# First phase of a decoder-layer kernel: a hand-written order, norm statistics by token, and low parts of the up weights on GpSimd

## The chip, the cores and the metric

The kernel runs on one core of a Trainium2 chip. The time is that of one execution on the device, in microseconds. The core has five engines that run side by side and wait for each other through semaphores: TensorE (PE, with its weight loads as PEld), VectorE (DVE), ScalarE (ACT), GpSimd (POOL) and SyncE (SP), which here only issues DMAs.

## What is computed

One decoder layer for 256 tokens of width 1024, in float32: a first feed-forward block, a mixer, a second feed-forward block, each with a norm modulated by a conditioning vector c. The change touches the beginning of the first feed-forward block alone:

```python
mod = silu(c) @ ada_w + ada_b                    # nine rows of 1024: sh1, sc1, g1, ...
n = x * rsqrt(mean(x * x, axis=-1) + EPS) * norm_ffn1_w
u = n * (1 + sc1) + sh1
gate, up = split(u @ ffn1_w_in, 2)               # ffn1_w_in: 1024 x 5632
h = x + 0.5 * g1 * ((silu(gate) * up) @ ffn1_w_out)
```

## The kernel before

**Layout and precision.** Activations lie with features on partitions: x is the tile h, 128 partitions x 8 slices x 256 tokens. A float32 product is made of three matmuls in a faster type. Each operand is split into a high part, rounded to that type, and a low part, the remainder (`half`: `act.copy(hi, v)` on ScalarE at line 128, the subtraction on VectorE at line 129). `mm3` then adds high x high (L137), low activation x high weight (L138) and high activation x low weight (L139). Weights, wst, come as high wh and low wl; activations u as uh and ul.

**The first phase** (tile pool `ep`) projects u onto the first seven tiles of 128 columns of the gate half and of the up half at once. It runs over the eight slices of 128 input features (`kt`). A slice needs two rows of ada_w of 512 KB each (`ada01`, for sc1 and sh1), and 2 x 896 weight columns, 896 KB (`w01`, gate columns at j = 0, up columns at j = 1). On VectorE, `ada_dots` (L181) multiplies such a row with silu(c), held on all partitions as cb, and sums it; `am` (L395) and `modc` (L398) are scale and shift of the slice, t (L401) is x times scale times the norm factor rb. ScalarE makes uh (L222), VectorE ul (L223). Then come 42 matmuls (seven tiles, gate and up, three each), into seven accumulators that stay open over all eight slices. wh and wl have four buffers each, two slices' worth; ada and wst four.

**Statistics and cb.** silu(c) is spread over partitions by products of ones with crow, the vector c on one partition (L362), and a silu from PSUM. For the norm, ScalarE squares x, VectorE adds the squares of all slices but for partitions (L378 to L382), a product with ones (L384) sums over partitions, ScalarE takes the root into rb (128 x 256), VectorE the reciprocal (L417). Between them stand products of ones with ones whose result nobody reads (`warm`, L368).

**What sets the order.** A scheduler with its own cost estimates sets every engine's order of instructions; the program text gives it only dependencies and priorities. SP's queue takes its loads in the order of the text. Behind the phase, silu(gate) * up is formed (L300), and the next weights are split by `half` for `pair_project`.

Of the kernel before, what the change touches and what calls it, by code (L numbers as in the profile page):

```python
# [32 lines left out]
V_N1, V_N2, V_N3, V_AB = 0, 8, 16, 24  # L33
# [10 lines left out]
HALF_BUFS = 4  # L44
SLOTS = 17
WIDE_BUFS = 3
F1 = 7
# [32 lines left out]
def layer(ctx: ExitStack, tc: tile.TileContext, a, out, packing):  # L80
    nc = tc.nc
    pe, act, dve = nc.tensor, nc.scalar, nc.vector

    cst = ctx.enter_context(tc.tile_pool(name="cst", bufs=1))
    wp = ctx.enter_context(tc.tile_pool(name="wp", bufs=1))
# [36 lines left out]
    def half(v):  # L122
        nk, n = v.shape[1], v.shape[2]
        hi = wp.tile([P, 1024], F32R, tag="wh", name=nm("wh"), bufs=HALF_BUFS)
        lo = wp.tile([P, 1024], F32R, tag="wl", name=nm("wl"), bufs=HALF_BUFS)
        hi = hi[:, :nk * n].rearrange("p (k n) -> p k n", k=nk)
        lo = lo[:, :nk * n].rearrange("p (k n) -> p k n", k=nk)
        act.copy(hi, v)  # L128
        last_lo[0] = dve.tensor_tensor(lo, v, hi.bitcast(F32), ALU.subtract).ins  # L129
        return hi, lo  # L130
# [5 lines left out]
    def mm3(o, l, r, first, last, skip=False):  # L136
        pe.matmul(o, l[0], r[0], start=first, stop=False, skip_group_check=skip)  # L137
        pe.matmul(o, l[0], r[1], start=False, stop=False, skip_group_check=skip)  # L138
        pe.matmul(o, l[1], r[0], start=False, stop=last, skip_group_check=skip)  # L139

    def at(pair, *idx):
        return pair[0][idx], pair[1][idx]
# [17 lines left out]
    def table(name):  # L160
        ins = act.preload_act_table_set(name).ins  # L161
# [12 lines left out]
    modc = cst.tile([P, N_MOD, KD], F32, name="modc")  # L174
# [4 lines left out]
    def ada_dots(st, j, f0):  # L179
        for i in range(st.shape[1]):  # L180
            dve.scalar_tensor_tensor(st[:, i, :], st[:, i, :], 1.0, cb, ALU.mult, ALU.mult,  # L181
                                     accum_out=raw[:, j, f0 + i:f0 + i + 1])
# [37 lines left out]
    def u_tile(u, f, t, jsh):  # L220
        sh = modc[:, jsh, f:f + 1]
        act.activation(u[0][:, f, :], t, AF.Identity, bias=sh)  # L222
        dve.scalar_tensor_tensor(u[1][:, f, :], t, sh, u[0][:, f, :].bitcast(F32),  # L223
                                 ALU.add, ALU.subtract)
# [109 lines left out]
                each()  # L334

    w1 = "ffn1_w_in"
    with tc.tile_pool(name="ep", bufs=1) as ep:
        table("silu_and_others")
        crow = ep.tile([1, D], F32, name="crow")
        nc.sync.dma_start(crow, a["c"])  # L340
# [17 lines left out]
        sts = [ada01(0)]  # L358
        wst = [w01(0)]
        for q in range(2):  # L360
            ps = misc_ps()
            pe.matmul(ps, ones[0:1, :], crow[:, q * 512:(q + 1) * 512], start=True, stop=True)  # L362
# [7 lines left out]
        warm(12)  # L370
        bias1 = ep.tile([P, KD], F32, name="bias1")
        dve.tensor_scalar(bias1, col[:, V_AB + KD:V_AB + 2 * KD], 1.0, None, ALU.add)
        table("sqrt_and_others")
        sqs = []
        for i in range(2):
            sq = ep.tile([P, 4, T], F32, tag="sq4", name=nm("sq4"), bufs=2)
            act.activation(sq, h[:, 4 * i:4 * i + 4, :], AF.Square)
            dve.tensor_tensor(sq[:, 0:2, :], sq[:, 0:2, :], sq[:, 2:4, :], ALU.add)  # L378
            sqs.append(sq)
        dve.tensor_tensor(sqs[0][:, 0:2, :], sqs[0][:, 0:2, :], sqs[1][:, 0:2, :], ALU.add)  # L380
        ssq = sqs[0][:, 0, :]
        dve.tensor_tensor(ssq, ssq, sqs[0][:, 1, :], ALU.add)  # L382
        ps = misc_ps()
        pe.matmul(ps[:, :T], ones, ssq, start=True, stop=True)  # L384
        rb = ep.tile([P, T], F32, name="rb")
        lookup(rb, ps[:, :T], AF.Sqrt, bias=epsc, scale=1.0 / D)
        warm(12)
        table("silu_and_others")
        u = new_u()
        am = sp.tile([P, KD], F32, tag="am", name=nm("am"), bufs=2)  # L390

        def u_first(kt, st, between=lambda: None):
            ada_dots(st[0], 1, kt)
            between()
            dve.scalar_tensor_tensor(am[:, kt:kt + 1], raw[:, 1, kt:kt + 1], bias1[:, kt:kt + 1],  # L395
                                     col[:, V_N1 + kt:V_N1 + kt + 1], ALU.add, ALU.mult)
            ada_dots(st[1], 0, kt)
            dve.tensor_tensor(modc[:, 0, kt:kt + 1], raw[:, 0, kt:kt + 1],  # L398
                              col[:, V_AB + kt:V_AB + kt + 1], ALU.add)
            t = ep.tile([P, T], F32, tag="t1", name=nm("t1"), bufs=2)  # L400
            dve.scalar_tensor_tensor(t, h[:, kt, :], am[:, kt:kt + 1], rb, ALU.mult, ALU.mult)  # L401
            u_tile(u, kt, t, 0)

        def halves(st):
            return [half(st[:, j:j + 1, :]) for j in range(2)]
# [5 lines left out]
        def first_mms(kt, j, hv):  # L411
            for f in range(F1):
                bank, slot_ = (banks[f // 2][j], f % 2) if f < 6 else (last, j)
                mm3(bank[:, slot_, :], at(hv, al, 0, slice(f * P, (f + 1) * P)), at(u, al, kt),
                    kt == 0 and slot_ == 0, kt == KD - 1 and slot_ == 1, skip=True)

        u_first(0, sts.pop(), lambda: dve.reciprocal(rb, rb))  # L417
        hw = halves(wst.pop())
        for kt in range(KD):
            if kt + 1 < KD:  # L420
                st = ada01(kt + 1)
                wt = w01(kt + 1)
                u_first(kt + 1, st)
                hw_next = halves(wt)
            first_mms(kt, 0, hw[0])
            first_mms(kt, 1, hw[1])
            hw = hw_next
    with tc.tile_pool(name=nm("fp"), bufs=1, reuse_waits="tile") as fp:
        ah = fp.tile([P, NF, T], F32R, name=nm("ah"))
# [6 lines left out]
        for p2 in range(4, NF // 2 + 1):  # L436
# [5 lines left out]
            else:  # L442
                ps = split_project(w1, f0 * P, FFN + f0 * P, u)
# [34 lines left out]
    with tc.tile_pool(name="mx", bufs=1, reuse_waits="tile") as mx:  # L478
# [385 lines left out]
    with tc.tile_pool(name=nm("fp"), bufs=1, reuse_waits="tile") as fp:  # L864
# [6 lines left out]
        for p2 in range(NF // 2):  # L871
# [14 lines left out]
            if p2 == 5:  # L886
# [104 lines left out]
```

## Time and profile before

| | us |
|---|---|
| median of 3 runs (lowest to highest) | 876.75 (876.51 to 878.15) |
| profiled execution, whole time | 876.71 |
| its span in the trace | 874.9 |
| first matmul of the phase (L137) starts | 18.10 |
| last matmul of the phase (L139) starts | 59.55 |
| mean granted TensorE clock over the span | 0.996 |

The span runs from the first to the last instruction of the program in the trace; the whole time lies 1.8 us above it. Rows of the timeline read: start, duration, engine, line, operation, output <- inputs, shapes, count, and in brackets the idle time of the engine before it and what ended it.

### The profile page before, as it was taken

The numbers are of one execution on the slowest core, as the hardware profiler recorded it, in microseconds if no ns is written. First come the engines' busy times: TensorE is split into PE (matmuls) and PEld (weight loads), VectorE is DVE, ScalarE is ACT, GpSimd is POOL, SyncE is SP. The second block draws the span as 40 slices with busy tenths as digits, with TensorE's granted clock in tenths as the row PEclk, the third lists the DMA queues.
The fourth block names the chain that finished last, engine by engine and source line by source line (L and its number), as shares of the span: only waits on it lengthen the run. The fifth ranks groups of instructions, "written<-read, shape, count | busy, mean of one in ns | idle before, by whom it ended". The sixth has DMA issues, their size and how long they took to land.

```text
span 874.9 us, 16783 instructions
## 1 busy us (share of the span) xinstructions
PE 861.0 (98%) x7038; PEld 843.6 (96%) x7038; DVE 663.8 (76%) x1000; ACT 505.5 (58%) x735; POOL 0.2 (0%) x4
## 2 busy tenths in 40 slices
PE   7999999999999999999999999999999999999996
PEld 6999999999999999999999999999999999999896
DVE  6989788897989858676898677866889985555454
ACT  5455454465666588858554558655557744444343
POOL 0000000000000000000000000000000000000000
PEclk9999999999999999999999999999999999999999
DMA  9958878994655334262757664464464685545531
GB/s 369 421 211 326 299 281 313 351 337 161 233 175 188 142 145 150 95 233 87 256 182 269 229 236 157 180 230 145 163 227 168 261 331 183 187 151 187 185 105 49
DMA packets 29023, 188.00 MB, mean 215 GB/s; under 512 B 3218, under 2 KB 3602, under 8 KB 9235
## 3 DMA queue, kind: packets, MB, share of 16 engines
q1 hardware_dynamic: 28658, 186.48, 58.3%
q8 instruction: 55, 0.90, 0.4%
q10 hardware_dynamic: 288, 0.44, 0.2%
q14 instruction: 22, 0.17, 0.1%
HBM read 185.86 MB, written 1.05 MB: 214 GB/s over the span
## 4 chain that ended last, share of the span: by engine, by line
PE 93%; DVE 4%; ACT 1%; DMA 1%; issue 1%; SPq 0%; DVEq 0%; ACTq 0%
PE proj L139 28%; PE proj L138 28%; PE proj L137 28%; PE misc L205 1%; DVE wl L129 1%; PE misc L137 1%; PE misc L139 1%; PE misc L138 1%; DMA ada<-in_ada_w_dram 1%; PE misc L676 1%; PE misc L652 0%; PE misc L805 0%; PE misc L640 0%; PE misc L806 0%; PE misc L807 0%
## 5 line engine op out<-in xcount | busy, mean ns | idle before, releaser
L128 ACT CAST wh<-wst 128x1024 fp32r<-128x1024 f32 (+3 forms) x282 | 288.9, 1032 | 280.7 <-PE proj L138 191.8
L129 DVE TENSOR_TENSOR wl<-wst,wh 128x1024 fp32r<-128x1024 f32 (+3 forms) x282 | 336.3, 1200 | 124.7 <-ACT wh L128 124.1
L137 PE MATMUL proj<-uh,wh 128*128 128x256 f32 (+1 forms) x1336 | 376.8, 283 | 2.3 <-ACT uh L222 2.3
L139 PE MATMUL proj<-uh,wl 128*128 128x256 f32 (+1 forms) x1336 | 377.4, 283 | 0.8 <-DVE wl L129 0.8
L138 PE MATMUL proj<-ul,wh 128*128 128x256 f32 (+1 forms) x1336 | 375.8, 282 | 0.0
L137 PEld LDWEIGHTS proj<-uh,wh 128*128 128x128 f32 x1336 | 250.9, 188 | 3.0 <-ACT uh L222 2.5
L139 PEld LDWEIGHTS proj<-uh,wl 128*128 128x128 f32 x1336 | 252.4, 189 | 1.2 <-DVE wl L129 1.0
L138 PEld LDWEIGHTS proj<-ul,wh 128*128 128x128 f32 x1336 | 252.3, 189 | 0.5 <-issue 0.2
L137 PE MATMUL proj<-s,wh 128*128 128x256 f32 x320 | 90.6, 284 | 0.2 <-ACT s L133 0.2
L139 PE MATMUL proj<-s,wl 128*128 128x256 f32 x320 | 89.6, 280 | 0.0
L138 PE MATMUL proj<-s,wh 128*128 128x256 f32 x320 | 89.3, 279 | 0.0
L181 DVE SCALAR_TENSOR_TENSOR wst<-wst,cb 128x1024 f32<-128x1024 f32 x56 | 67.4, 1220 | 7.2 <-DMA wst<-in_ada_w_dram 6.9
L137 PEld LDWEIGHTS proj<-s,wh 128*128 128x128 f32 x320 | 60.1, 188 | 1.0 <-issue 0.5
L138 PEld LDWEIGHTS proj<-s,wh 128*128 128x128 f32 x320 | 60.2, 188 | 0.3 <-issue 0.2
L139 PEld LDWEIGHTS proj<-s,wl 128*128 128x128 f32 x320 | 60.2, 188 | 0.2 <-issue 0.2
L139 PE MATMUL proj<-ah,wl 128*128 128x256 f32 x176 | 49.1, 279 | 0.0
L137 PE MATMUL proj<-ah,wh 128*128 128x256 f32 x176 | 49.1, 279 | 0.0
L138 PE MATMUL proj<-al,wh 128*128 128x256 f32 x176 | 49.1, 279 | 0.0
L138 PE MATMUL proj<-wl,ah 128*128 128x256 f32 (+1 forms) x132 | 42.1, 319 | 0.0
L139 PE MATMUL proj<-wh,al 128*128 128x256 f32 (+1 forms) x132 | 42.1, 319 | 0.0
L137 PE MATMUL proj<-wh,ah 128*128 128x256 f32 (+1 forms) x132 | 42.1, 319 | 0.0
L161 ACT ACT_TABLE_LOAD x28 | 35.9, 1283 | 1.2 <-PEq L965 0.7
(224 smaller groups left out, 1134.4 us busy)
## 6 DMA issues: line engine op xcount, KB each, us to landing
wst<-in_mix_w_in_dram SPq DMA_DIRECT2D x52, 1024.0 KB, 4.9
wst<-in_ffn_w_in_dram SPq DMA_DIRECT2D x37, 1024.0 KB, 5.2
wst<-in_ada_w_dram SPq DMA_DIRECT2D x28, 1024.0 KB, 5.9
wst<-in_ffn_w_out_dram SPq DMA_DIRECT2D x17, 1024.0 KB, 4.9
ada<-in_ada_w_dram SPq DMA_DIRECT2D x16, 512.0 KB, 11.7
wst<-in_w_br_ssd_dram SPq DMA_DIRECT2D x8, 1024.0 KB, 4.9
wst<-in_w_br_ret_dram SPq DMA_DIRECT2D x8, 1024.0 KB, 5.0
wst<-in_ffn_w_in_dram SPq DMA_DIRECT2D x7, 896.0 KB, 12.3
```

The source lines that it names most:

```text
L128: act.copy(hi, v)
L129: last_lo[0] = dve.tensor_tensor(lo, v, hi.bitcast(F32), ALU.subtract).ins
L137: pe.matmul(o, l[0], r[0], start=first, stop=False, skip_group_check=skip)
L138: pe.matmul(o, l[0], r[1], start=False, stop=False, skip_group_check=skip)
L139: pe.matmul(o, l[1], r[0], start=False, stop=last, skip_group_check=skip)
L161: ins = act.preload_act_table_set(name).ins
L181: dve.scalar_tensor_tensor(st[:, i, :], st[:, i, :], 1.0, cb, ALU.mult, ALU.mult, accum_out=raw[:, j, f0 + i:f0 + i + 1])
L205: pe.matmul(ps[:, :T], mean_m[n], s, start=i == 0, stop=i == len(parts) - 1)
L676: pe.matmul(py[hh * 64:hh * 64 + 64, f * T + c * P:f * T + (c + 1) * P], xd[:, c, hl * 64:hl * 64 + 64], m[c][:, hl, :], start=True, stop= ...
```

## The change

Inside the first phase the order of TensorE, ScalarE, VectorE and SyncE is that of the text (`tc.manual_schedule`); GpSimd is not among them. Behind the phase the scheduler works as before.

- x is loaded first; c comes as 128 copies straight into cb, whose silu is taken in place. The identity (ident) is loaded early on ScalarE's queue.
- The loads of three slices are issued ahead of the loop, then of slice kt + 3 in step kt.
- Statistics: each block of squares, 128 features x 128 tokens, is the stationary side of a product with a column of 1/1024, so that the mean squares stand with tokens on partitions, two columns in all. Root and reciprocal work on those; dg = ident * r, and a product of ones with dg spreads the factor over partitions again. Slice 0 reads it from PSUM, the others from rb, a copy.
- In a slice, the low part of the up weights (j = 1) is subtracted by GpSimd instead of VectorE (`lows`).

```diff
-    with tc.tile_pool(name="ep", bufs=1) as ep:
+    with (tc.tile_pool(name="ep", bufs=1) as ep,
+          tc.manual_schedule(engines={e.engine for e in (pe, act, dve, nc.sync)})):
...
-        nc.sync.dma_start(crow, a["c"])
         act.dma_start(col, a["vecs"])
+        act.dma_start(ident, a["consts"][:, :P])
...
+        nc.sync.dma_start(cb, a["c"].broadcast_to([P, D]))
...
-            pe.matmul(ps, ones[0:1, :], crow[:, q * 512:(q + 1) * 512], start=True, stop=True)
-            lookup(cb[:, q * 512:(q + 1) * 512], ps, AF.Silu)
...
+        for kt in range(3):
+            sts.append(ada01(kt))
+            wst.append(w01(kt))
...
+        warm(8)
...
             act.activation(sq, h[:, 4 * i:4 * i + 4, :], AF.Square)
-            dve.tensor_tensor(sq[:, 0:2, :], sq[:, 0:2, :], sq[:, 2:4, :], ALU.add)
...
-        pe.matmul(ps[:, :T], ones, ssq, start=True, stop=True)
...
+            for f in range(4):
+                for tt in range(2):
+                    pe.matmul(ps[:, tt:tt + 1], sq[:, f, tt * P:(tt + 1) * P], mean1,
...
+        lookup(cb, cb, AF.Silu)
+        warm(5)
...
+        def lows(kt, hw, j):
+            (nc.gpsimd if j else dve).tensor_tensor(hw[1][j], wst[kt][:, j, :], hw[0][j].bitcast(F32), ALU.subtract)
...
+        scale_first(0)
+        r = ep.tile([P, 2], F32, name="r2")
+        table("sqrt_and_others")
+        lookup(r, ps[:, :2], AF.Sqrt, bias=epsc)
+        dve.reciprocal(r, r)
+        dg = ep.tile([P, 2, P], F32, name="dg")
+        dve.tensor_tensor(dg, ident.unsqueeze(1).broadcast_to([P, 2, P]),
+                          r.unsqueeze(2).broadcast_to([P, 2, P]), ALU.mult)
+        ps = misc_ps()
+        for tt in range(2):
+            pe.matmul(ps[:, tt * P:(tt + 1) * P], ones, dg[:, tt, :], start=True, stop=True)
+        warm(10)
+        shift_first(0)
+        hw = halves(0)
...
+        t = t_first(0, ps[:, :T])
+        act.copy(rb, ps[:, :T])
+        table("silu_and_others")
+        lows(0, hw, 0)
+        u_low(0, t)
+        lows(0, hw, 1)
...
         for kt in range(KD):
+            if kt + 3 < KD:
+                sts.append(ada01(kt + 3))
+                wst.append(w01(kt + 3))
             if kt + 1 < KD:
...
+                hw_next = halves(kt + 1)
+                scale_first(kt + 1)
+                shift_first(kt + 1)
+                t = t_first(kt + 1, rb)
+                lows(kt + 1, hw_next, 0)
+                u_low(kt + 1, t)
+                lows(kt + 1, hw_next, 1)
+            first_mms(kt, 0, hw)
+            first_mms(kt, 1, hw)
```

`scale_first` is the first dot and am, `shift_first` the second dot and modc, `halves` the two casts to wh, `t_first` t and uh, `u_low` ul.

TensorE at the start of the program, before; numbers behind names tell buffers apart:

```order
L362 MATMUL misc_97<-crow,ones 128x512
L362 MATMUL misc_100<-crow,ones 128x512
L368 MATMUL misc_103<-ones 128x128 x12
L384 MATMUL misc_127<-sq_6_119,ones 128x256
L368 MATMUL misc_131<-ones 128x128 x12
L137 MATMUL proj_148<-uh_145,wh_164 128x256
L137 MATMUL proj_150<-uh_145,wh_164 128x256
```

and TensorE at the same place now, with the first rows of slice 0:

```order
L362 MATMUL misc_111<-ones 128x128 x8
L377 MATMUL misc_120<-mean_109,sq_9_121 128x1 x8
L377 MATMUL misc_120<-mean_109,sq_10_131 128x1 x8
L362 MATMUL misc_142<-ones 128x128 x5
L428 MATMUL misc_161<-dg,ones 128x128 x2
L362 MATMUL misc_164<-ones 128x128 x10
L137 MATMUL proj_192<-uh_150,wh_177 128x256
L138 MATMUL proj_192<-ul_151,wh_177 128x256
L139 MATMUL proj_192<-uh_150,wl_178 128x256
```

The products with crow are gone, the one product for the statistics became sixteen of one column, and slice 0 no longer begins with seven products that need neither ul nor wl: L138 is second.

VectorE from the first dot to the first t, before:

```order
L181 SCALAR_TENSOR_TENSOR ada_91,raw<-ada_91,cb 128x1024
L378 TENSOR_TENSOR sq_7_122<-sq_7_122 128x512
L395 SCALAR_TENSOR_TENSOR am_147<-raw,bias_116,col 128x1
L380 TENSOR_TENSOR sq_6_119<-sq_6_119,sq_7_122 128x512
L181 SCALAR_TENSOR_TENSOR ada_91,raw<-ada_91,cb 128x1024
L382 TENSOR_TENSOR sq_6_119<-sq_6_119 128x256
L398 TENSOR_TENSOR modc<-raw,col 128x1
L129 TENSOR_TENSOR wl_165<-wst_94,wh_164 128x896
L129 TENSOR_TENSOR wl_169<-wst_94,wh_168 128x896
L417 RECIPROCAL rb<-rb 128x256
L181 SCALAR_TENSOR_TENSOR ada_172,raw<-ada_172,cb 128x1024
L401 SCALAR_TENSOR_TENSOR t_20_160<-h,am_147,rb 128x256
```

and VectorE at the same place now, up to ul of slice 0:

```order
L181 SCALAR_TENSOR_TENSOR ada_93,raw<-ada_93,cb 128x1024
L389 SCALAR_TENSOR_TENSOR am_152<-raw,bias_148,col 128x1
L422 RECIPROCAL r_155<-r_155 128x2
L424 TENSOR_TENSOR dg<-k,r_155 128x256
L181 SCALAR_TENSOR_TENSOR ada_93,raw<-ada_93,cb 128x1024
L394 TENSOR_TENSOR modc<-raw,col 128x1
L436 SCALAR_TENSOR_TENSOR t_21_184<-h,am_152,misc_161 128x256
L409 TENSOR_TENSOR wl_178<-wst_96,wh_177 128x896
L441 SCALAR_TENSOR_TENSOR ul_151<-t_21_184,modc,uh_150 128x256
```

The sums of squares, one low part and the next slice's dot no longer stand ahead of t, and the reciprocal has 2 columns instead of 256.

VectorE's last slice and what follows it, now:

```order
L409 TENSOR_TENSOR wl_573<-wst_454,wh_572 128x896
L441 SCALAR_TENSOR_TENSOR ul_151<-t_73_582,modc,uh_150 128x256
L129 TENSOR_TENSOR wl_705<-wst_701,wh_704 128x1024
L300 TENSOR_TENSOR s_680<-s_680,proj_193 128x512
L300 TENSOR_TENSOR s_685<-s_685,proj_195 128x512
```

Before, there were two low parts to a slice, and the two L300 stood ahead of the first low part of the next weights (L129, 128x1024); now that low part is first.

More of the change, by code (lines that the diff above doesn't have):

```diff
@@ L368, in warm @@
                 pe.matmul(ps[:, :P], ones, ones, start=True, stop=True)
[L370 to L374, printed above, removed]
+        sts, wst = [], []
+        for kt in range(3):
+            sts.append(ada01(kt))
+            wst.append(w01(kt))
+        mean1 = ep.tile([P, 1], F32, name="mean1")
+        dve.memset(mean1, 1.0 / D)
+        warm(8)
+        ps = misc_ps()
         for i in range(2):
@@ L386, in layer @@
[L386 to L388 removed]
+            for f in range(4):
+                for tt in range(2):
+                    pe.matmul(ps[:, tt:tt + 1], sq[:, f, tt * P:(tt + 1) * P], mean1,
+                              start=i == f == tt == 0, stop=i == 1 and f == 3 and tt == 1,
+                              skip_group_check=True)
+        lookup(cb, cb, AF.Silu)
+        warm(5)
+        bias1 = ep.tile([P, KD], F32, name="bias1")
@@ L398, in u_first, with halves @@
             dve.tensor_tensor(modc[:, 0, kt:kt + 1], raw[:, 0, kt:kt + 1],
                               col[:, V_AB + kt:V_AB + kt + 1], ALU.add)
+        def halves(kt):
+            st = wst[kt]
+            his, los = [], []
+            for j in range(2):
+                his.append(wp.tile([P, 1024], F32R, tag="wh", name=nm("wh"), bufs=HALF_BUFS))
+                los.append(wp.tile([P, 1024], F32R, tag="wl", name=nm("wl"), bufs=HALF_BUFS))
+            his, los = ([t[:, :F1 * P] for t in x] for x in (his, los))
+            for j in range(2):
+                act.copy(his[j], st[:, j, :])
+            return his, los
@@ new lines, in lows, with first_mms @@
+        def lows(kt, hw, j):
+            (nc.gpsimd if j else dve).tensor_tensor(hw[1][j], wst[kt][:, j, :], hw[0][j].bitcast(F32), ALU.subtract)
+        def first_mms(kt, j, hw):
+            hv = hw[0][j], hw[1][j]
+            for f in range(F1):
+                bank, slot_ = (banks[f // 2][j], f % 2) if f < 6 else (last, j)
+                mm3(bank[:, slot_, :], at(hv, al, slice(f * P, (f + 1) * P)), at(u, al, kt),
+                    kt == 0 and slot_ == 0, kt == KD - 1 and slot_ == 1, skip=True)
@@ L400, in u_first, with t_first @@
+        warm(10)
+        shift_first(0)
+        hw = halves(0)
+        rb = ep.tile([P, T], F32, name="rb")
+        def t_first(kt, rb):
             t = ep.tile([P, T], F32, tag="t1", name=nm("t1"), bufs=2)
             dve.scalar_tensor_tensor(t, h[:, kt, :], am[:, kt:kt + 1], rb, ALU.mult, ALU.mult)
-            u_tile(u, kt, t, 0)
-        def halves(st):
-            return [half(st[:, j:j + 1, :]) for j in range(2)]
+            act.activation(u[0][:, kt, :], t, AF.Identity, bias=modc[:, 0, kt:kt + 1])
+            return t
```

37 lines of the change are left out of this document (9 added, 28 removed).

## The prediction

> **What bounds the kernel now.** I read the page first, then the waits of TensorE, then the chain that ended last, then stretches of the timeline.
>
> ```profile
> PE 861.0 (98%) x7038; PEld 843.6 (96%) x7038; DVE 663.8 (76%) x1000; ACT 505.5 (58%) x735; POOL 0.2 (0%) x4
> PE 93%; DVE 4%; ACT 1%; DMA 1%; issue 1%; SPq 0%; DVEq 0%; ACTq 0%
> PE misc L362 <- DMA crow<-in_c_dram: 2.4, 1, 2.4
> PE proj L137 <- ACT uh L222: 2.3, 1, 2.3
> PE misc L384 <- DVE modc L398: 0.9, 1, 0.9
> PE proj L139 <- DVE wl L129: 0.8, 1, 0.8
> ```
>
> TensorE is busy for 98% of the span and 93% of the chain is its matmuls. Its waits of 0.8 us and more number four, and all four lie at the start or at the end of the first phase. A shorter time can therefore come only from an earlier first useful matmul, from fewer slow matmuls behind it, or from the wait of 0.8. The chain shows what holds the first matmul back.
>
> ```profile
> 2.00 6.12 DMA ada<-in_ada_w_dram
> 8.23 1.23 DVE ada L181 x2
> 10.80 1.15 DVE ada L181 x2
> 12.35 1.33 DVE wl L129 x2
> 14.27 1.75 DVE rb L417
> 16.02 1.09 DVE ada L181 x2
> ```
>
> After the first conditioning rows have landed, VectorE carries everything: two dots, the sums of squares between them, two low parts, a reciprocal of 1.75, and a dot that belongs to the *next* slice. The reader sees a queue in a poor order, not a lack of data.
>
> ```profile
> 6.04:11.43 5.39, 5.39 (x25) 5.19 (x24) 3.86 (x7) 3.87 (x4) 0.00 (x0) 1.00 1.02 410
> 12.93:15.78 2.85, 2.85 (x25) 2.65 (x23) 2.85 (x3) 1.76 (x2) 0.00 (x0) 1.00 0.99 413
> 18.10:21.70 3.60, 3.60 (x17) 3.60 (x18) 3.60 (x8) 2.08 (x3) 0.00 (x0) 0.53 0.99 412
> 21.70:50.00 28.30, 28.30 (x240) 28.30 (x239) 28.24 (x52) 12.18 (x16) 0.00 (x0) 1.00 0.98 404
> ```
>
> The columns are the stretch, its length, busy time and count of PE, PEld, DVE, ACT and POOL, the granted clock, the DMA share and GB/s. The first two stretches hold the same filler: 24 or so passes take 5.39 us, then 2.85, so a pass costs 0.21 or 0.11 us. The first 3.6 us of useful work run at a granted clock of 0.53: 17 matmuls, 0.21 us each, against 28.30/240 = 0.118 later. These 17 would have taken 2.0 us, so the slow stretch costs **1.6 us**.
>
> ```profile
> 21.95 1.22 DVE L181 SCALAR_TENSOR_TENSOR ada<-ada,cb 128x1024 f32<-128x1024 f32 x1
> 26.39 1.09 DVE L129 TENSOR_TENSOR wl<-wst,wh 128x896 fp32r<-128x896 f32 x1
> 27.40 1.22 DVE L181 SCALAR_TENSOR_TENSOR ada<-ada,cb 128x1024 f32<-128x1024 f32 x1
> 49.18 1.22 DVE L181 SCALAR_TENSOR_TENSOR ada<-ada,cb 128x1024 f32<-128x1024 f32 x1
> 18.10 0.67 PE L137 MATMUL proj<-uh,wh 128*128 128x256 f32 x2 [2.32 <-ACT uh L222]
> 59.55 0.28 PE L139 MATMUL misc<-uh,wl 128*128 128x256 f32 x1
> 60.86 0.39 PE L139 MATMUL proj<-uh,wl 128*128 128x256 f32 x1 [0.79 <-DVE wl L129]
> ```
>
> From slice 2 (21.95) to slice 7 (49.18) VectorE needs 27.23/5 = 5.45 us a slice, with no gap (28.24 of 28.30 us busy). TensorE needs 42 x 0.118 = 4.95. VectorE is thus the slower one, and only its lead keeps TensorE fed. An earlier start of TensorE alone would soon run into it. The second low part takes 27.40 - 26.39 = 1.01 of the 5.45; without it VectorE needs **4.44**, below TensorE.
>
> **The change, part by part.** The inputs come first.
>
> ```profile
> 0.73 0.35 SPq L340 DMA_DIRECT2D crow<-in_c_dram  x1
> 1.14 0.82 SPq L112 DMA_DIRECT2D h<-in_x_dram  x2
> 4.93 1.05 ACT L377 ACTIVATE sq<-h 128x1024 f32<-128x1024 f32 x1
> 10.50 0.94 ACT L128 CAST wh<-wst 128x896 fp32r<-128x896 f32 x1 [1.39 <-DMA wst<-in_ffn_w_in_dram]
> 11.62 0.94 ACT L128 CAST wh<-wst 128x896 fp32r<-128x896 f32 x1 [0.18 <-DMA wst<-in_ffn_w_in_dram]
> 17.54 0.51 ACT L222 ACTIVATE uh<-t,modc 128x256 fp32r<-128x256 f32 x1 [2.63 <-DVE t L401]
> 18.69 0.48 DVE L223 SCALAR_TENSOR_TENSOR ul<-t,modc,uh 128x256 fp32r<-128x256 f32 x1
> DMA packets 2947, 12.61 MB, mean 420 GB/s; under 512 B 324, under 2 KB 324, under 8 KB 2945
> wf<-in_norm_final_w_dram SPq DMA_DIRECT2D x1, 512.0 KB, 6.2
> h<-in_x_dram SPq DMA_DIRECT2D x2, 512.0 KB, 4.5
> 13.63 1.28 ACT L161 ACT_TABLE_LOAD   x1
> ```
>
> Without crow ahead, x goes out 0.41 us earlier. The vector c now arrives as 128 copies, 512 KB; at 420 GB/s that is 1.25 us, and it stands ahead of all weights. The one load of that form, wf, landed 6.2 us after its issue, the halves of x, as large, after 4.5; I take the 1.25 and keep 1.7 more as its upper end. Everything behind it is later by 1.25 - 0.41 = 0.84: the weight casts start at 11.34 and 12.46, the second ends at 13.4. ScalarE's order puts uh of slice 0 behind it, so uh runs from 13.4, the first matmul follows 0.56 later as at 17.54 and 18.10, and ul, behind uh, is done at 14.4. The extra load of ident, 64 KB on ScalarE's queue, is 0.15 us by the same rate. TensorE, held to the written order, takes L138 second and needs ul then: it cannot flow before **14.4**.
>
> The rest must be ready by then. The dot starts when its rows land, 8.23 + 0.84 = 9.1, and ends 1.2 later; the reciprocal of 1.75 shrinks to two columns, the sums of squares leave VectorE, and the second dot ends at about 12.2. VectorE is no longer last. ScalarE gets c's copies 1.25 before the rows, at 7.9; their silu (like a square, 1.05) and the table of 1.28 bring it to the root at 10.2. TensorE's own queue is the tight one: 8 fillers, 16 products of one column, 5 fillers, 2 products with dg, 10 fillers. A filler is two passes.
>
> ```profile
> 2.36 3.75 PE L362 MATMUL misc<-crow,ones 1*128 1x512 f32 x4 [2.36 <-DMA crow<-in_c_dram]
> 292.20 0.53 PE L607 MATMUL misc<-av,k 128*128 128x32 f32 x4
> 292.56 0.39 PE L610 MATMUL misc<-av,ones 128*128 128x32 f32 x2
> ```
>
> The nearest row for the one-column products has 32 columns: four passes start within 0.36 us at full speed, 0.09 to 0.11 each, as much as a filler of 128, so the load of the stationary tile sets it. At the slow pace it is between that (if the load keeps its speed) and double. Thirty-two passes are 3.2 us fast and up to 6.4 slow. The fillers start at 2.35, where TensorE starts now, and end 16 x 0.21 later, near 5.9; x is squared by then (4.93 - 0.41 + 1.05 = 5.6). If the pace rises as before, after 5.4 us of work, at 7.8, nine passes are slow and 23 fast: the statistics end at 10.2, five fillers at 11.3, the products with dg at 11.8, ten fillers at **14.1**. Root, reciprocal and dg, of 2, 2 and 256 columns (ul's 256 took 0.48), fit beside the five fillers. So the first matmul runs at about 14.1, the flow starts at 14.6 with a little slack added, and it starts fast. TensorE's gain is 18.1 - 14.6 = 3.5 and the slow stretch, 1.6.
>
> The matmuls of slice 0 lose nothing else: before, seven L137 were put ahead to hide ul's lateness, now the fillers hide it. If they were too few, TensorE would idle at most from 14.1 to 14.4.
>
> GpSimd then has one low part a slice, which no row of this trace shows.
>
> ```profile
> L129 DVE TENSOR_TENSOR wl<-wst,wh 128x896 fp32r<-128x896 f32 x16 | 17.3, 1088 | 0.1
> L417 DVE RECIPROCAL rb<-rb 128x256 f32<-128x256 f32 x1 | 1.7, 1747 | 0.0
> ```
>
> The nearest row is the same subtraction on VectorE, 1.09 us; the farthest is the slowest rate per column on the page, the reciprocal's 1.747/256, which gives 6.1 for 896. I take something near the first, up to twice it: by its place, anything below TensorE's 4.95 a slice is hidden, since the product that needs it stands 21 matmuls (2.5 us) after the first of its slice. The Trainium skill, GPSIMD Engine Reference, section "Elementwise — side-by-side cycle accounting", gives 4497 ns for such an instruction of 2048 columns; an estimate by it is 1.97 us here, hidden too, and no run here shows it.
>
> At the end of the phase the wait of 0.79 had VectorE behind two swiglu products. In the new order the first low part of the next weights stands ahead of them, and VectorE comes with a lead; I count 0.5 of the 0.79 and keep 0 and 0.79 as its bounds. Beyond it TensorE waits no more, so what is gained stays gained. The data allow it: the loads of the phase are 1.9 MB a slice, 4.5 us at 420 GB/s, below 4.95.
>
> Sum against the profiled execution, 876.71 (span 874.9 and 1.8 around it, 0.04 below the median of 876.75): 876.71 - 3.5 - 1.6 - 0.5 = 871.1; I say **871.2**.
>
> **The rivals.** *VectorE stands still while GpSimd reads (slower).* Every large VectorE instruction of the phase reads two tiles. If it and GpSimd's subtraction exclude each other, each slice costs 4.44 + s, s being the time GpSimd holds it. Slice 0 is ready at 14.4 + s, slice 7 seven paces later, at 45.5 + 8s, and its 42 matmuls end 4.95 later. Before, the phase's last matmul started at 59.55, 0.118 more ends it, and 0.79 was lost behind it: 60.5. The two meet at s = 1.26, hardly above VectorE's own 1.09; there it decides. With s = 2 the end is at 66.4: 876.71 + 5.9 = **882.6**; with 2.2, 884.2. For it: VectorE has no slack to give. Against it: nothing, since GpSimd does nothing in this trace; 0.33, with the case of GpSimd alone near 6 us (8 x 6.1 behind 13.4, then half a slice: 64.7, +4.2) in it. The Trainium skill, SBUF — State Buffer, section "Who interferes with whom", says exactly this: a VectorE instruction with two SBUF inputs contends with a GpSimd instruction that reads SBUF, and whichever comes second is blocked for the whole of the first. With the 1.97 above its time would be 882.4. No run here shows it yet.
>
> *The one-column products stay slow.* If they don't raise TensorE's pace, statistics end at 5.9 + 6.4 = 12.3, five fillers at 14.4, dg at 15.3, ten fillers (20 passes, part of them fast) at 18.5 to 19.5. The first matmul is 0.9 later than now, but fast: 876.71 + 0.9 - 1.6 - 0.5 = **875.5**. For it: in the stretch from 6.04 the passes stayed slow for 5.4 us though TensorE had been busy since 2.36 with products of one row, which seem not to count. Against it: one-column products use all rows. 0.22. The Trainium skill, TensorE: Matmul & The Clock Gate, section "What's actually happening", has the clock at half until a free-running window of about 3.4 us was busy; the trace agrees within two windows, and that page does not settle whether loads of the stationary tile count.
>
> *It doesn't do what it says:* the order shows that it does.
>
> **How the numbers follow.** Forecast 0.45 (870.3 with all of the 0.79 and a little less at the start, to 873.5 with none of it and the 1.7 of c's copies), slow statistics 0.22, standstill 0.33. The measurement tells about 0.2%, 1.75 us. Faster by more: 0.45 + 0.03 of the second case = 0.48; same: 0.19 of it; slower: 0.33. The range goes from 870.3, the forecast's lower end, to 884, which leaves only the worst standstill out.
>
> **What would show it.** Right: first L137 by 15, granted clock 1.00 behind it, VectorE's slice at or below 4.6 with gaps, no TensorE wait on GpSimd. Standstill: dots or low parts of VectorE that last 2 us and more or start late, 6 us a slice, TensorE waiting on wl. Slow statistics: L377 lasting 6 us, first L137 near 19. The forecast fails, too, if c's 128 copies land later than 1.3 us behind x.

## The result, and the profile after

The changed kernel took **884.25 us** (median of 4 runs, 883.13 to 885.0); the kernel before, beside it on the same chip, 877.17 (4 runs, 876.51 to 878.15). The ratio is 1.0082, 95% interval 1.0070 to 1.0094: slower by 7 us. The profiled execution is one of the four, 884.23, with a span of 882.4 (874.9 before).

| us in the profiled execution | before | after |
|---|---|---|
| first matmul of the phase starts | 18.10 | 18.11 |
| last matmul of the phase starts | 59.55 | 67.91 |
| lost by TensorE right behind it | 0.79 | none |
| VectorE, one slice | 5.45 | 6.26 |

The phase ends 8.36 - 0.79 = 7.57 later, the span is 7.5 longer: all of it was lost inside the phase, and behind it nothing was won or lost. First the page's engine row and the shares of the chain, then TensorE's three largest waits up to 80 us (engine, line, what it waited for: total, times, longest).

```profile
PE 866.8 (98%) x7066; PEld 849.3 (96%) x7066; DVE 666.8 (76%) x990; ACT 505.5 (57%) x735; POOL 17.7 (2%) x12
PE 89%; DVE 7%; ACT 1%; DMA 1%; issue 1%; DVEq 0%; ACTq 0%; SPq 0%
```

```profile
PE proj L138 <- DVE ul L441: 3.8, 8, 0.5
PE proj L137 <- ACT uh L437: 1.9, 7, 0.4
PE misc L377 <- ACT sq L374: 1.2, 1, 1.2
```

VectorE's part of the chain went from 4% to 7%. TensorE now waits in every one of the eight slices, for ul, and in seven for uh, and never for GpSimd's low part, which the waits don't name. So GpSimd is in time; what is late is VectorE. The timeline of slice 2 shows why (start, duration, engine, line, operation):

```profile
25.24 1.21 DVE L181 SCALAR_TENSOR_TENSOR ada<-ada,cb 128x1024 f32<-128x1024 f32 x1
...
26.21 2.22 POOL L409 TENSOR_TENSOR wl<-wst,wh 128x896 fp32r<-128x896 f32 x1 [2.57 <-ACT wh L405]
26.50 1.95 DVE L389 SCALAR_TENSOR_TENSOR am<-raw,bias,col 128x1 f32<-128x1 f32 x1
28.37 1.21 DVE L181 SCALAR_TENSOR_TENSOR ada<-ada,cb 128x1024 f32<-128x1024 f32 x1
...
31.50 1.22 DVE L181 SCALAR_TENSOR_TENSOR ada<-ada,cb 128x1024 f32<-128x1024 f32 x1
```

`am` makes one number per partition and takes 0.22 us by itself. Here it lasts 1.95 and ends, with the next instruction's start at 28.37, when GpSimd's subtraction does (26.21 + 2.22 = 28.43). The slice takes 31.50 - 25.24 = 6.26. The groups up to 68 us (busy us, mean ns) show which instructions were hit over the whole phase:

```profile
L389 DVE SCALAR_TENSOR_TENSOR am<-raw,bias,col 128x1 f32<-128x1 f32 x8 | 12.1, 1517 | 0.3
L436 DVE SCALAR_TENSOR_TENSOR t<-h,am,rb 128x256 f32<-128x256 f32 x7 | 5.2, 746 | 0.0
L394 DVE TENSOR_TENSOR modc<-raw,col 128x1 f32<-128x1 f32 x8 | 3.1, 391 | 0.3
```

The start, in the timeline of the same kernel:

```profile
1.05 3.79 PE L362 MATMUL misc<-ones 128*128 128x128 f32 x16 [1.05 <-DVE mean L369]
6.00 6.99 PE L377 MATMUL misc<-mean,sq 128*128 128x1 f32 x32 [1.17 <-ACT sq L374]
12.85 2.48 PE L362 MATMUL misc<-ones 128*128 128x128 f32 x10
13.03 0.26 ACT L169 ACTIVATE r<-misc,epsc 128x2 f32<-128x2 f32 x1 [2.78 <-PE misc L377]
15.12 2.00 DVE L394 TENSOR_TENSOR modc<-raw,col 128x1 f32<-128x1 f32 x1
18.44 0.47 DVE L441 SCALAR_TENSOR_TENSOR ul<-t,modc,uh 128x256 fp32r<-128x256 f32 x1
18.97 0.39 PE L138 MATMUL proj<-ul,wh 128*128 128x256 f32 x1 [0.48 <-DVE ul L441]
```

The 32 passes of the statistic stayed slow to the last: 6.99/32 = 0.218 us each. The eight fillers ahead of them had run out at 4.84, 1.2 us before the first squares were there. The root waited 2.78 for the passes. Then `modc` of slice 0 met GpSimd's first subtraction (2.00 instead of 0.16), and ul of slice 0 came at 18.9.

So two suspects stand in the trace: **A**, GpSimd's reading holds VectorE; **B**, the new order with its slow statistics. The runs put a price on each.

### The profile page after: what moved, and what is told of

Its sections match the earlier page's. It is cut to its first block, busy times and chain, and to the rows that moved or that the text cites. A ratio compares the mean times of both kernels' runs of the same rounds, so it can differ in the third digit from the quotient of the medians.

```text
span 882.4 us, 16840 instructions
## 1 busy us (share of the span) xinstructions
PE 866.8 (98%) x7066; PEld 849.3 (96%) x7066; DVE 666.8 (76%) x990; ACT 505.5 (57%) x735; POOL 17.7 (2%) x12
## 3 DMA queue, kind: packets, MB, share of 16 engines
HBM read 186.45 MB, written 1.05 MB: 212 GB/s over the span
## 4 chain that ended last, share of the span: by engine, by line
PE 89%; DVE 7%; ACT 1%; DMA 1%; issue 1%; DVEq 0%; ACTq 0%; SPq 0%
PE proj L139 27%; PE proj L138 27%; PE proj L137 27%; DVE ada L181 2%; PE misc L205 1%; DVE am L389 1%; DVE wl L129 1%; DVE wl L409 1%; PE misc L377 1%; PE misc L716 1%; DVE t L436 1%; DMA wst<-in_ffn_w_in_dram 1%; PE misc L139 0%; PE misc L138 0%; PE misc L137 0%
## 5 line engine op out<-in xcount | busy, mean ns | idle before, releaser
L128 ACT CAST wh<-wst 128x1024 fp32r<-128x1024 f32 (+2 forms) x266 | 274.5, 1039 | 273.6 <-PE proj L138 199.7
L129 DVE TENSOR_TENSOR wl<-wst,wh 128x1024 fp32r<-128x1024 f32 (+2 forms) x266 | 319.2, 1207 | 127.4 <-ACT wh L128 126.9
L138 PE MATMUL proj<-ul,wh 128*128 128x256 f32 (+1 forms) x1336 | 376.4, 282 | 3.8 <-DVE ul L441 3.8
L138 PEld LDWEIGHTS proj<-ul,wh 128*128 128x128 f32 x1336 | 251.8, 188 | 5.9 <-DVE ul L441 5.4
L138 PE MATMUL proj<-s,wh 128*128 128x256 f32 x320 | 89.3, 279 | 0.0
L138 PEld LDWEIGHTS proj<-s,wh 128*128 128x128 f32 x320 | 60.2, 188 | 0.3 <-issue 0.2
L138 PE MATMUL proj<-al,wh 128*128 128x256 f32 x176 | 49.1, 279 | 0.0
L138 PE MATMUL proj<-wl,ah 128*128 128x256 f32 (+1 forms) x132 | 42.1, 319 | 0.0
## 6 DMA issues: line engine op xcount, KB each, us to landing
ada<-in_ada_w_dram SPq DMA_DIRECT2D x16, 512.0 KB, 10.2
```

## Experiments

Times are medians; ratios are to the kernel before, run on the same chip between the others (its medians there were 876.2 to 876.8).

**1. The low parts back on VectorE, the rest as changed.**

```diff
-            (nc.gpsimd if j else dve).tensor_tensor(hw[1][j], wst[kt][:, j, :], ...)
+            dve.tensor_tensor(hw[1][j], wst[kt][:, j, :], ...)
```

> The changed kernel with one part undone: the low parts of the up weights are subtracted on VectorE again, the new order stays. Theory 'VectorE is held while GpSimd reads' (A): VectorE goes at its old 5.45 us a slice instead of 6.26; ul of slice 0 is done at about 18.2, ul of slice 7 at 56.3, the phase ends 4.95 later or a little after, at 61.3 to 62.5 instead of 68.0; time 877.9 to 879.0, so some 6 us come back and about 1 us stays with the late statistics. Theory 'the new order and the slow statistics cost the 7 us' (B): the time stays at 883 or above. No gain, no loss of a third kind is expected: behind the phase nothing differs.

Measured 878.12, ratio 1.0020 (1.0011 to 1.0030); the phase's last matmul starts at 60.65. Six of the seven us come back. (The phase itself ends about half a us earlier than A's 61.3; TensorE loses 0.8 waiting for a low part at 184 us, far behind it.) The groups up to 60 us:

```profile
L389 DVE SCALAR_TENSOR_TENSOR am<-raw,bias,col 128x1 f32<-128x1 f32 x8 | 1.8, 220 | 0.3
L436 DVE SCALAR_TENSOR_TENSOR t<-h,am,rb 128x256 f32<-128x256 f32 x7 | 3.3, 478 | 0.0
L394 DVE TENSOR_TENSOR modc<-raw,col 128x1 f32<-128x1 f32 x8 | 1.3, 159 | 0.3
```

The same instructions at their own length. The difference to the three rows of the changed kernel, 10.3 + 1.9 + 1.8 = 14.0 us, is what GpSimd took from VectorE: **1.75 us a slice**, for a low part that cost VectorE 1.01. VectorE's slice here is 5.54; 5.54 - 1.01 + 1.75 = 6.28, as seen.

**2. GpSimd alone, in the kernel before.**

```diff
-            return [half(st[:, j:j + 1, :]) for j in range(2)]
+            return [half(st[:, 0:1, :]), half(st[:, 1:2, :], nc.gpsimd)]
```

> The kernel before with the other part alone: the low parts of the up weights are subtracted on GpSimd, the order of the phase stays the scheduler's. A (VectorE is held): the pace becomes about 6.2 us a slice instead of 5.45, and seven to eight slices of it cost 5 to 6 us: 881.5 to 884. B (order and statistics cost it): the low part leaves VectorE, TensorE becomes the bound with 4.95 a slice, 0 to 2 us faster than before: 875 to 877.

Measured 886.68, ratio 1.0123 (1.0104 to 1.0141): A, and worse than its upper end. A group of VectorE from 19 to 56 us, then a row of GpSimd's timeline:

```profile
L181 DVE SCALAR_TENSOR_TENSOR ada<-ada,cb 128x1024 f32<-128x1024 f32 x10 | 21.5, 2175 | 0.0
```

```profile
34.60 2.17 POOL L129 TENSOR_TENSOR wl<-wst,wh 128x896 fp32r<-128x896 f32 x1 [5.19 <-ACT wh L128]
```

Here it is a dot that is held: 2.18 on the mean instead of 1.22. GpSimd's subtractions follow each other every 7.36 us, 1.1 more than in the changed kernel, since in this order the two casts stand behind uh on ScalarE, and VectorE waits for them and for uh as well.

**3. No low parts of the up weights.**

```diff
-            (nc.gpsimd if j else dve).tensor_tensor(hw[1][j], wst[kt][:, j, :], ...)
+            if j == 0:
+                dve.tensor_tensor(hw[1][j], wst[kt][:, j, :], ...)
```

> Leaves out the low parts of the up weights altogether (their products read a tile of zeros), in the new order; no engine subtracts them. A: VectorE needs 4.44 us a slice, TensorE 4.95 and is the bound; with ul of slice 0 at about 18.2 the phase ends at 57.0 to 57.8, against 60.5 before and 68.0 in the changed kernel; time 873.5 to 874.6. B: 882 or above.

The products that need this low part read a tile of zeros instead, filled once at the start. Measured 874.77, ratio 0.9974 (0.9965 to 0.9983): 0.2 above the range given for A and far from B. VectorE's slice is 4.53 (22.90 to 27.43), near the forecast's 4.44. TensorE is busy for 10.00 of 10 us in each window from 20 to 60; it is the bound.

**4. GpSimd writes only.** As 3, and GpSimd fills the staged up weights with zeros.

```diff
+            if j:
+                nc.gpsimd.memset(wst[kt][:, j, :], 0.0)
```

> As the kernel without low parts of the up weights (they are left out here too), but GpSimd writes zeros into the staged up weights after their cast: eight instructions of the same shape that read nothing. If it is GpSimd's reading that holds VectorE (A, narrow): like the kernel without them, 873.5 to 875. If any instruction of GpSimd holds it (A, wide): with a price of 1 us each VectorE needs 5.44 a slice and the time is about 877.5, with 2 us 6.44 and about 884.

Measured 874.55, ratio 0.9975 (0.9963 to 0.9987). The group of GpSimd, then two of VectorE up to 56 us:

```profile
L415 POOL MEMSET wst<- 128x896 f32 x8 | 6.8, 848 | 42.6 <-ACT wh L410 42.6
```

```profile
L417 DVE TENSOR_TENSOR wl<-wst,wh 128x896 fp32r<-128x896 f32 x8 | 8.7, 1086 | 0.9 <-ACT wh L410 0.9
L449 DVE SCALAR_TENSOR_TENSOR ul<-t,modc,uh 128x256 fp32r<-128x256 f32 x8 | 3.9, 484 | 0.5 <-ACT uh L445 0.3
```

Eight instructions of GpSimd of 0.85 us lie beside VectorE's low parts, ul and dots, and these keep their length. One fill runs from 25.46 to 26.31, beside a low part (24.59, 1.09 long), ul (25.84, 0.48) and the start of a dot (26.24, 1.22). Writing alone holds nothing.

**5. GpSimd reads one operand.**

```diff
+            if j:
+                nc.gpsimd.tensor_copy(hw[1][j], wst[kt][:, j, :])
```

> GpSimd copies the staged up weights into the tiles of their low parts instead of subtracting, so the up weights' low parts are wrong, and GpSimd reads one operand instead of two. If one operand read is enough to hold VectorE for the whole copy (estimate from the eight zero fills of this shape, 0.85 us each, up to the subtraction's 2.1): pace 4.44 + 0.85 to 2.1, 5.3 to 6.5 a slice, time 877.5 to 884. If only an instruction with two operands read holds it, VectorE needs 4.44, TensorE's 4.95 is the bound: as the kernel without these low parts, 873.5 to 875.5.

The copies are of whole weights, so this kernel too leaves out the low parts of the up weights. Measured 874.28, ratio 0.9977 (0.9966 to 0.9987), inside the range given for "only two operands hold it". But the time misleads here. The groups of VectorE up to 56 us:

```profile
L389 DVE SCALAR_TENSOR_TENSOR am<-raw,bias,col 128x1 f32<-128x1 f32 x8 | 4.5, 559 | 0.3
L394 DVE TENSOR_TENSOR modc<-raw,col 128x1 f32<-128x1 f32 x8 | 3.1, 386 | 0.3
```

Against 1.8 and 1.3, VectorE lost 2.7 + 1.8 = 4.5 us, 0.56 a slice. Without the second low part its slice is 4.53 (run 3) against TensorE's 4.95, so it has 0.42 a slice and its lead to give, and the end didn't move. One operand read does hold VectorE, for less; run 12 makes that visible in the time.

**6. A quarter of the statistic's products**, the rest as changed.

```diff
-            for f in range(4):
+            for f in range(1):
```

> The changed kernel with 4 instead of 16 of the products that sum the squares, so three quarters of the mean square are left out. Theory: the 32 slow passes (0.213 us each) made the statistics end at 13.0; with 8 of them they end near 8, the root is at about 10.4, and slice 0 has ul at about 16 instead of 18.9. GpSimd still holds VectorE, so the pace stays 6.26 and the 3 us pass straight to the end: 880.5 to 881.7. If the statistics were hidden behind something else (rows of the modulation, casts), nothing changes: 883.5 to 884.7.

This leaves three quarters of the mean square out. Measured 882.25, ratio 1.0073 (1.0057 to 1.0089): 2.0 us come back, not 3; as a ratio, 1.0073 after 1.0082, the step is not clear of the noise. The pace stays 6.26. ul of slice 0, with GpSimd's first subtraction beside it, and one of TensorE's waits over the whole span:

```profile
14.45 2.22 DVE L441 SCALAR_TENSOR_TENSOR ul<-t,modc,uh 128x256 fp32r<-128x256 f32 x1
PE proj L139 <- DVE wl L129: 1.5, 2, 0.8
```

ul ends at 16.7 instead of 18.9. It would have been earlier still, but GpSimd's subtraction held ul itself (2.22 instead of 0.48), and the fillers held TensorE until 16.66 as well. The last matmul of the phase starts at 65.86 instead of 67.91, 2.05 earlier. The profiled execution is the slowest of the four (884.33; the others 882.17 to 882.25): it loses the gain again at 186 and 190 us, far behind the phase, where TensorE waits for low parts as the second row shows.

**7. Both out:** 3 and 6 together.

> Both suspected costs out: a quarter of the statistic's products, and no low parts of the up weights (both left out of what is computed). This is the case that the prediction forecast. If the two causes are all that stood against it: ul of slice 0 at about 14.5, TensorE the bound from there with 4.95 a slice, 870.8 to 871.6, or up to 872.8 if the first matmuls still meet the slow clock. If a third cause exists: 873.5 or more.

Measured 872.70, ratio 0.9958 (0.9941 to 0.9974): at the upper edge of what was expected with no third cause. The timeline shows what is left:

```profile
12.64 4.35 PE L362 MATMUL misc<-ones 128*128 128x128 f32 x20
14.36 0.48 DVE L447 SCALAR_TENSOR_TENSOR ul<-t,modc,uh 128x256 fp32r<-128x256 f32 x1
16.75 0.36 PE L137 MATMUL proj<-uh,wh 128*128 128x256 f32 x1
```

All inputs of slice 0 are there by 14.8, and TensorE is still at fillers, 20 slow passes, until 16.7.

**8. Both out, and 22 fillers at the start instead of 8.**

> The kernel with both suspected costs out (a quarter of the statistic's products, no low parts of the up weights) took 872.7, not the forecast 871.2: in its profile ul of slice 0 is done at 14.8, but the ten fillers ahead of the first useful matmul run slow (20 passes in 4.35 us) and end at 16.8. Here the first group of fillers is 22 instead of 8, so that TensorE is busy without a gap from 1.04 to about 8. Theory 'the slow clock of the fillers is the rest': the granted clock is full before 10, the ten fillers take 2.3 us, the useful matmuls flow from 14.3 to 14.9: 870.5 to 871.5. If the fillers are not what holds it: 872.3 to 873.1 as before.

Measured 873.37, ratio 0.9967 (0.9956 to 0.9978): expected 870.5 to 871.5, a miss. By the noise it is no different from run 7, and near the rival's 872.3 to 873.1: the fillers were not what held the end. The clock was full from 6.4, the fillers fast, and the first useful matmul came 2.45 earlier, at 14.30. The last of the phase came only 0.48 earlier (56.14 against 56.62). The timeline:

```profile
12.05 2.40 PE L362 MATMUL misc<-ones 128*128 128x128 f32 x20
...
17.54 1.78 ACT L410 CAST wh<-wst 128x896 fp32r<-128x896 f32 x2 [1.73 <-DMA wst<-in_ffn_w_in_dram]
23.49 1.79 ACT L410 CAST wh<-wst 128x896 fp32r<-128x896 f32 x2 [3.76 <-DMA wst<-in_ffn_w_in_dram]
```

The casts of slices 1 and 2 wait for their weights; TensorE, early now, stops just before 20.3 for ul, and from 25.2 to 26.3 for uh and ul behind them. With the wait for ul in slice 0 that is some 2 us. The loads are the third bound of this phase.

**9. All low parts and the sums of squares on VectorE**, in the new order.

```diff
+            dve.tensor_tensor(sq[:, 0:2, :], sq[:, 0:2, :], sq[:, 2:4, :], ALU.add)
...
+        for tt in range(2):
+            pe.matmul(ps[:, tt:tt + 1], ssq[:, tt * P:(tt + 1) * P], mean1, ...)
```

> The whole computation, in the new order, with two changes back: all low parts on VectorE, and the squares summed on VectorE in its idle time before the first rows land, so that 2 products instead of 16 make the statistic. The gain of the statistics (about 3 us by theory) on top of the kernel with all low parts on VectorE (878.1): 873.4 to 875.4, faster than both kernels. If the statistics cost nothing: 878.

Measured 876.14, ratio 0.9997 (0.9988 to 1.0006). The statistics are worth 2.0 here as well (878.12 to 876.14), a us less than expected. TensorE waits for ul in slices 3 to 7: VectorE's 5.5 us a slice is again what ends last.

**10. A rebalanced start:** 9, with `am` and `modc` on ScalarE, 25 fillers at the start (6 and 8 further on), TensorE's products ordered so that the low weights are needed last, and ScalarE's casts of the next slice's weights moved from ahead of `am` to behind it.

```diff
+            act.activation(am[:, kt:kt + 1], raw[:, 1, kt:kt + 1], AF.Identity, bias=bias1[:, kt:kt + 1],
+                           scale=col[:, V_N1 + kt:V_N1 + kt + 1])
...
+            for a_, b_, j in ((0, 0, 0), (0, 0, 1), (0, 1, 0), (0, 1, 1), (1, 0, 0), (1, 0, 1)):
```

> The whole computation, built from what the other runs showed, to beat both kernels. All low parts on VectorE; the squares summed on VectorE in its idle time; am and modc of a slice, two instructions of 0.22 and 0.16 us, on ScalarE; TensorE takes the products of a slice in the order uh.wh, ul.wh, uh.wl, so that the low parts are needed last; 25 fillers at the start instead of 8, 6 and 8 later. If VectorE's work a slice sets the end (theory): pace about 5.2 instead of 5.45, last low part at about 52 to 53, and TensorE, busy from about 14, ends the phase at 53.5 to 55 instead of 60.5: 870 to 872. If the am and modc across engines cost more in waiting than they save: 874 to 876, as the kernel with the sums on VectorE (876.1) or little better.

Measured 876.26, ratio 1.0001 (0.9991 to 1.0010): the rival. TensorE flows from 13.9, but the waits show a new one:

```profile
PE proj L424 <- ACT uh L449: 2.9, 7, 1.2
PE proj L139 <- DVE wl L129: 1.3, 2, 0.8
```

From slice 2 on ScalarE makes both casts between `am` and uh, uh is late, VectorE's ul behind it too, and the pace is 5.50. The second row lies behind the phase, at 179 and 183 us, and is a wait that the kernel before doesn't have there.

**11. The casts ahead of `am`** from slice 3 on; in slice 2 the second cast goes behind t.

```diff
+                if not late:
+                    cast(kt + 1, hw_next, 0)
+                    cast(kt + 1, hw_next, 1)
                 scale_first(kt + 1)
```

> As the rebalanced kernel (876.3), with one order changed on ScalarE: there the two casts of a slice, 1.78 us, stood between am and uh from the third slice on, uh came 0.3 to 0.5 us too late for VectorE, and TensorE waited for uh 0.5 us a slice (2.9 us in all). From slice 3 on both casts now stand ahead of am. Theory: VectorE goes at 5.1 to 5.2 us a slice without a gap, TensorE waits for uh no more behind slice 2, the phase ends at about 55.5 instead of 58.8, and the time is 872.5 to 874. If VectorE's pace is set by something else: 875.5 to 877.

Measured 875.04, ratio **0.9977** (0.9968 to 0.9987): faster than the kernel before by 0.2%, but 1 us above the range. The pace is 5.09 as forecast, and the last matmul starts at 56.76 instead of 58.7. TensorE's waits up to 300 us, then a dot behind the phase here and the same dot in the kernel before:

```profile
PE proj L424 <- ACT uh L449: 2.2, 2, 1.9
PE proj L139 <- DVE wl L129: 1.8, 2, 1.0
```

```profile
175.05 1.22 DVE L181 SCALAR_TENSOR_TENSOR wst<-wst,cb 128x1024 f32<-128x1024 f32 x1 [2.58 <-DMA wst<-in_ada_w_dram]
176.05 1.23 DVE L181 SCALAR_TENSOR_TENSOR wst<-wst,cb 128x1024 f32<-128x1024 f32 x1 [0.26 <-DMA wst<-in_ada_w_dram]
```

1.9 are lost in slice 1, whose weights land too late for a start at 13.5, and 1.8 far behind the phase, at 177 and 181 us, where TensorE waits for low parts; before, that wait isn't there. VectorE's order at that place is the same in both kernels. But here VectorE stands idle for 2.58 us until rows of ada_w have landed, before for 0.26, and the low parts stand behind that dot. Why the rows aren't there sooner stays open.

**12. GpSimd makes the casts of the up weights** in kernel 11.

```diff
-            act.copy(hw[0][j], wst[kt][:, j, :])
+            (nc.gpsimd.tensor_copy if j else act.copy)(hw[0][j], wst[kt][:, j, :])
```

> As the kernel with the casts first, but GpSimd makes the casts of the up weights instead of ScalarE: an instruction with one operand read, as the copies that cost the phase nothing. If GpSimd holds VectorE only where it reads two operands: VectorE keeps its pace of 5.1 to 5.2, ScalarE has 0.9 us less a slice, and the time is that of the kernel with the casts first or up to 0.5 less. If one operand held it after all where VectorE has no slack (1 to 1.9 us for each of eight casts, the bounds of the copies): 8 us more, 880 or above.

Measured 877.48, ratio 1.0006 (0.9997 to 1.0015): 2.4 slower than 11, between the two expectations. The timeline:

```profile
28.44 1.89 POOL L415 CAST wh<-wst 128x896 fp32r<-128x896 f32 x1 [2.72 <-DVE wl L418]
29.46 1.94 DVE L181 SCALAR_TENSOR_TENSOR ada<-ada,cb 128x1024 f32<-128x1024 f32 x1
...
31.73 1.08 DVE L418 TENSOR_TENSOR wl<-wst,wh 128x896 fp32r<-128x896 f32 x1
37.56 1.08 DVE L418 TENSOR_TENSOR wl<-wst,wh 128x896 fp32r<-128x896 f32 x1
```

The dot lasts 1.94 instead of 1.22, and the pace is 37.56 - 31.73 = 5.83 instead of 5.09. This slice is one of several between 5.1 and 6.4. Over the phase (groups up to 56 us) VectorE's dots take 1.4 us more than in run 11, t 2.0 and ul 1.4, together 4.8: a cast, one operand read, holds VectorE for 0.6 us on the mean. TensorE's waits for uh grow from 2.2 to 4.9. GpSimd itself ran the same form in 0.94 at 19.21, where VectorE was idle, and needs up to 1.9 elsewhere. The rows fit its waiting for VectorE first: the cast from 28.44 lies beside a dot that ends near 29.5, and 0.9 more ends it. That is inferred from the times, not shown.

## Why the prediction was wrong

Medians of the runs, by what was left in; in brackets the start of the phase's last matmul in the profiled execution:

| us | 16 statistic products | 4 of them, or 2 behind sums on VectorE (middle row) |
|---|---|---|
| low part of the up weights on GpSimd | 884.25 (67.91) | 882.25 (65.86) |
| on VectorE | 878.12 (60.65) | 876.14 (59.48) |
| left out | 874.77 (58.91) | 872.70 (56.62) |

The two causes about add up: the statistics cost 2.0 to 2.1 us in every row, GpSimd 6.1 against VectorE in both columns. That the medians agree to a tenth is closer than the runs allow: executions of one kernel lie 0.8 to 2.8 us apart, and only in the middle row are the two ratios clear of each other. The phase's end, read from the traces, moves by 2.05, 1.17 and 2.29 for the statistics, and by 7.26 and 6.38 for GpSimd against VectorE.

**The step that failed: "anything below TensorE's 4.95 a slice is hidden".** It priced GpSimd's low part by its own length and the place where its result is needed. By that measure it was right: it took 2.08 to 2.23, and TensorE never waited for it. But it took 1.75 of VectorE's time while saving 1.01, and so VectorE's slice went to 6.26, not to 4.44. Run 1 removes just this and gets 6.1 us back; run 2 adds just this and loses 10; runs 4 and 12 show that it is GpSimd's reading that does it. The sum of the forecast has no term for GpSimd: it stands there at nothing, with "GpSimd does nothing in this trace" as the whole evidence. Measured, the term is 884.25 - 874.77 = 9.5 against leaving the low part out. This was the slower rival, given 0.33 against the forecast's 0.45. Its formula had the right parts: 4.44 + s a slice, s between 1.75, what VectorE lost, and 2.2, GpSimd's own length; it decides from 1.26. It put the phase's end at 66.4 for s = 2; with good statistics, in run 6, it is 65.86 + 0.12 = 66.0. The Trainium skill, SBUF — State Buffer, section "Who interferes with whom", states that a VectorE instruction with two SBUF inputs contends with a GpSimd instruction that reads SBUF, not with one that only writes it. Runs 1, 2, 4 and 12 agree: two-input VectorE instructions (`am`, 128 x 1, 1.52 us on the mean instead of 0.22, as well as the dots, 128 x 1024, 2.18 instead of 1.22) were held by GpSimd's reads, and low parts, ul and dots kept their length beside its writes.

**The second term mis-sized: statistics that end at 10.2.** They ended at 12.99; the pace never rose under them. Forecast were 4.3 us for them (5.9 to 10.2), measured 7.0 (6.00 to 12.99). The root came 2.8 late, and the first useful matmul at 18.11, not 14.1. The fillers ahead of them need no data and began at 1.05, not 2.35; so they had run out before x was squared. In the five executions profiled with these 16 products they ended at 10.91 (run 4), 11.46 (run 5), 11.72 (run 1), 12.99 (changed kernel) and 13.33 (run 3): fast passes at first where the clock had risen early, slow ones behind, and in none did the passes bring the clock up. This was the other rival, given 0.22; without GpSimd's part its price, 875.5, is near run 3's 874.77. As a price in the end it is the 2 us of the table. The rivals were written as alternatives, and both happened; the first rival's 882.6 was for a good start, which run 6 gives (882.25). Both together are 884.25, just above the range's 884.

From the forecast's 871.2 the way is thus 1.5 us for what it had too good by itself (below), 2.1 for the statistics and 9.5 for GpSimd, 13 in all.

**Right:** ScalarE's silu of cb starts at 7.89 (7.9 forecast), the first dot at 9.23 (9.1), the first useful matmuls run at the full clock (the 1.6 forecast for that was gained), and TensorE's 0.79 behind the phase is gone. These gains are real, but from slice 1 on VectorE's 6.26 a slice sets the end, and each slice gives back 6.26 - 4.95 = 1.3 us of them.

**The forecast's own case** was too good by 1.5 to 2.2 us: 871.2 against 872.70 and 873.37 in runs 7 and 8. Two steps failed there. The fillers were counted at a fast pace that the clock did not have in run 7; and "the data allow it" compared rates, 4.5 us of loads against 4.95 of matmuls, where the weights of slices 1 and 2 come too late for a start at 14.3.

## What to carry to other kernels

Work moved to an idle engine is priced by what it takes from the engine it is meant to relieve, not by whether its own result is in time: here 1.75 us taken for 1.01 saved. Where two engines' bounds nearly coincide (5.45 and 4.95 a slice), ask of each moved instruction which of the two it slows. And an experiment on an engine with slack can hide a cost: read the durations of the instructions beside it (run 5), not the time alone.

## What the runs showed of the hardware

A product with a one-column moving side does not hold TensorE's clock up. Windows of the kernel with GpSimd's copies (length, busy time and count of PE, PEld, DVE, ACT, POOL, then the granted clock), and its statistics in the timeline:

```profile
4.44:7.86 3.42, 2.06 (x18) 1.86 (x18) 0.17 (x1) 2.11 (x2) 0.00 (x0) 1.00 0.96 365
7.86:14.68 6.82, 6.82 (x34) 6.82 (x34) 3.95 (x8) 4.47 (x5) 1.44 (x1) 0.50 1.03 422
14.68:18.00 3.32, 3.32 (x31) 3.32 (x31) 3.27 (x6) 2.54 (x4) 0.46 (x1) 1.00 1.00 417
```

```profile
6.07 5.38 PE L377 MATMUL misc<-mean,sq 128*128 128x1 f32 x32 [1.36 <-ACT sq L374]
11.32 2.48 PE L362 MATMUL misc<-ones 128*128 128x128 f32 x10
```

The clock rose at 4.44 and fell to half at 7.86; the stretch between had a gap (TensorE was idle from 4.71 to 6.07), so the fall alone says nothing of the passes. The next window does: from 7.86 to 11.27 it was filled by one-column passes without a gap, and the clock did not rise at its end. It rose at 14.68, one window of fillers and dg products later. In the changed kernel the passes run from 6.00 to 12.99 and the clock rises only at 15.83 (a pass takes 0.21 us ahead of it and 0.12 behind), so a whole window of them, 9.00 to 12.42, counted for nothing there as well. A window filled with one-column passes thus counts as not busy.

The Trainium skill, TensorE: Matmul & The Clock Gate, section "What's actually happening", has the window free-running and about 3.4 us long. The trace agrees with that length: the clock changes 3.42 and 6.82 = twice 3.41 apart.

The moment of the first rise differs between executions that start TensorE alike. With the same eight fillers it came at 4.11 (run 1), 4.44 (run 5), 5.47 (run 4), 15.83 (changed kernel) and 17.50 (run 3). So a chain of fillers that is just long enough is fast in one run and slow in the next.
